# One block of GLA, NSA and SwiGLU: buffers of FFN and down projection laid at 160 and 224 modulo 256, plain weight tiles by token halves, and single products cut in two

## The chip, the cores and the metric

The kernel runs on one core of one Trainium2 chip. The metric is the device time of one execution in microseconds; the number used is the median of three runs.

## The reference, cut to what matters

One decoder block over x with 512 tokens and 1024 features, in float32:

```python
h = rms_norm(x, norm_mix_pre)
proj = h @ w_in                       # split into GLA q, k, v, r, a; NSA q, k, v; gates; merge gates
o_gla, o_nsa = gla_mixer(...), nsa_mixer(...)
mixed = sigmoid(merge_gla) * (o_gla @ w_proj_gla) + sigmoid(merge_nsa) * (o_nsa @ w_proj_nsa)
x = x + rms_norm(mixed @ w_out, norm_mix_post)
h = rms_norm(x, norm_ffn_pre)
f = (silu(h @ w_ffn_gate) * (h @ w_ffn_up)) @ w_ffn_down      # 1024 -> 2816 -> 1024
x = x + rms_norm(f, norm_ffn_post)
```

GLA is a chunked gated linear attention with 4 heads, NSA an attention with 8 heads over compressed blocks, selected blocks and a window. Neither changes here.

## The kernel before, in words

All activations lie transposed, features on the 128 partitions and the 512 tokens along the free dimension. The dense products run in float32r with a split: each weight and each activation is a high part and a low part (`whi`, `wlo`; `hT_hi`, `hT_lo`), and one block of 128x128 weights gives three matmuls, high by high, high by low, low by high, summed in a PSUM bank. Below, "product" is one such matmul.

**Plain tiles.** A tile of 128 output features is eight blocks k = 0 to 7 of 128 input features, so 24 products, each over all 512 tokens (`prod`, lines 177 to 186). These are: eight tiles of q, k and merge gates at the start (`qa`, from `with_gla`), run in pieces of one block with side work between; six of `with_cmp`; 19 of `with_att`, which are fed into the gaps of the attention; the tile T_MB+7; eight tiles `pb` of half the depth (12 products); output projection tiles 0 to 2; gate and up tile 2 of the FFN (`third`); and eight tiles of the down projection over its last eight blocks of hidden features, with bank `acc` and `tp` in turn and the forms of the next stage as side work (`side`).

**By halves already.** Output tiles 3 to 7 (`out_half`) and gate and up tiles 0 and 1 (`ffn_half`) run for 256 tokens at a time.

**Units.** The other dense layers use a 2x2 scheme with seven instead of eight block products (Strassen's, in Winograd's form): nine pairs of input tiles (`eproduct`), 19 units of gate and up tile n = 3 to 21 (`unit`, N0 = 3), and four units of the down projection over 14 blocks (`down_product`). Their products are all 256 columns wide: 12 in each of the seven block products of a pair or a unit, 21 in those of down. The sums of weight quarters and of token halves, and their split into high and low parts (`dform`, `x_form`, `split_pair`), are DVE's and ACT's work beside the products.

**What sets the order.** The code calls the steps in a hand-made order; a scheduler then orders each engine's instructions by readiness and the code's order, so products of neighbouring steps may be interleaved. Each engine runs its own queue in order. PSUM has banks of four names (`mm`, `sc`, `acc`, `tp`), two of each; a bank is free when the engine that evacuates it is done. Weights come by DMA on SP's queue into `wraw`, are split by ACT and DVE, and one tile ahead is asked for (`Stream`).

**Where buffers lie.** SBUF pools hand out addresses one after the other, in the order of the requests. A tile of 16 floats (`half_line`) shifts all that follows by 64 bytes. "At 160" means that a buffer's address in its partition is 160 modulo 256 bytes. Before, `hT` and the inputs of pairs and units begin at 160 and their weights at 224, except for some buffers of FFN and down: the two last parts of `h2l`, `t2` and parts of `b11` and `t1` of down lie at 224 as moving operands, and the weights of output tile 7 and `u2` (`w_e`) lie at 160.

Of the kernel before, what the change touches and what calls it, by code (L numbers as in the profile page):

```python
# [16 lines left out]
S = 512  # L17
# [77 lines left out]
def hybrid_block_kernel(ctx: ExitStack, tc: tile.TileContext, I, outT):  # L95
# [78 lines left out]
    ALL = slice(0, S)  # L174

    def prod(ps, w, xh, xl, k0, kn, ktot, t=ALL):

        wh, wl = w
        marks = []
        for kk in range(kn):  # L180
            k = k0 + kk
            c = slice(kk * 128, (kk + 1) * 128)
            pe.matmul(ps[:, t], wh[:, c], xh(k)[:, t], start=(k == 0), stop=False)  # L183
            pe.matmul(ps[:, t], wh[:, c], xl(k)[:, t], start=False, stop=False)  # L184
            marks.append(pe.matmul(ps[:, t], wl[:, c], xh(k)[:, t], start=False, stop=(k == ktot - 1)))  # L185
        return marks
# [39 lines left out]
    halves = (slice(0, S // 2), slice(S // 2, S))  # L226
# [86 lines left out]
    def eplace(u, a):  # L313
# [5 lines left out]
        if a == "a22" and u + 1 < NU:  # L319
            if u == 0:  # L320
                half_line(mid)
            return [mid.tile([128, S], F32R, tag="kst" + x, name="ek" + x) for x in "sw"]
# [56 lines left out]
    def eproduct(u, i):  # L379
# [11 lines left out]
        for q in range(4):  # L391
            c = slice(q * 128, (q + 1) * 128)
            for m, (w, x) in enumerate(((wh, xh), (wh, xl), (wl, xh))):
                pe.matmul(o, w[:, c], x[q], start=(first and q == 0 and m == 0), stop=(q == 3 and m == 2),  # L394
                          skip_group_check=True)
# [288 lines left out]
    class Pieces:  # L684


        def __init__(self, keys):
            self.it = (None for key in keys for _ in self.one(key))

        def one(self, key):  # L690
# [79 lines left out]
    qa = Pieces(with_gla)  # L770
# [6 lines left out]
    gates_log(AF.Exp, stk["abs"], scale=-1.0)  # L777
    first = pair(0, (15, 16), (3, 5))
# [12 lines left out]
    mid2 = p_mid2.__enter__()  # L791
    p_nsa = tc.tile_pool(name="nsa", bufs=1, reuse_waits="tile")
# [334 lines left out]

    weave(runs(with_cmp[:2]), [])
# [13 lines left out]
    mix2 = p_mix2.__enter__()  # L1142
    run(("h", T_MB + 7))
# [28 lines left out]
    early = [flat(quad("e%d" % i, F32, "early%d" % i)) for i in range(2)]  # L1172

# [3 lines left out]
    def w_slot(which):  # L1177
# [4 lines left out]
        tags = {"d0": ("d0h", "d0l"), "d1": ("d1h", "d1l"), "c": ("hl2", "hl3"), "u": ("uu", "uu"), "g3": ("g3h", "g3l"), "rw": ("rw", "rw")}[which]  # L1182
# [5 lines left out]
    rs = []  # L1188

    def w_e():  # L1190
        if not rs:
            rs.append(ffn.tile([128, 48], F32, name="rs3"))
# [4 lines left out]
    h2h, h2l = quads("h2h", 4, F32R, "hh"), quads("h2l", 2, F32R, "hl")  # L1197
    rs1, rs2 = [ffn.tile([128, NT], F32, name=x) for x in ("rs1", "rs2")]
    h2l += [quad("hl%d" % i, F32R, "h2l%d" % i) for i in (2, 3)]
# [72 lines left out]
    def ffn_half(e, w, ps, ks=range(KD)):  # L1272
# [3 lines left out]
        for k in ks:  # L1276
            i, j = k // 2, k % 2
            c = slice(k * 128, (k + 1) * 128)
            for x in range(2):
                wh, wl = w[x]  # L1280
                o = ps[x][:, t]
                pe.matmul(o, wh[:, c], h2h[i][:, j, t], start=(k == 0), stop=False)
                pe.matmul(o, wh[:, c], h2l[i][:, j, t], start=False, stop=False)
                last = pe.matmul(o, wl[:, c], h2h[i][:, j, t], start=False, stop=(k == KD - 1))
# [144 lines left out]
    def unit(n, between=None):  # L1429
# [7 lines left out]
        def product(o, a, b, first):  # L1437
            (ah_, al_), (bh_, bl_) = forms.pop((n, a)), XF[b]
            for q in range(4):
                c = slice(q * 128, (q + 1) * 128)  # L1440
                for i, (w, x) in enumerate(((ah_, bh_), (ah_, bl_), (al_, bh_))):
                    pe.matmul(o, w[:, c], x[q], start=(first and q == 0 and i == 0), stop=(q == 3 and i == 2),  # L1442
                              skip_group_check=True)
# [13 lines left out]

        product(r1, "a11", "b11", True)
# [36 lines left out]
    def dform(name, room_for, src, t):  # L1495
        cols = [x if len(x.shape) == 2 else flat(x) for x in room_for]
        at = [x[:, c:c + 512] for x in cols for c in range(0, x.shape[1], 512)]
# [18 lines left out]
    half_line(ffn)  # L1516
    w0 = (st.next(("g", 0)), st.next(("u", 0)))
    for n in BYHALF:
# [77 lines left out]
    with tc.issue_after(stk["last"].ins):  # L1596
# [7 lines left out]
    dform("b11", [quad("sa", F32R, "db11_%d" % i) for i in range(2)] + [quad("rw", F32R, "db11_%d" % i) for i in (2, 3)],  # L1604
          left, h0)
    t2d = [quad("g3h", F32, "dt2_0"), quad("g3l", F32, "dt2_1")]
    for i in range(4):
        dve.tensor_tensor(out=half_of(t2d, i), in0=left(i, h1), in1=left(i, h0), op=OP.add)
# [8 lines left out]
    def sub_t2(of, t, by):  # L1617
        for i in range(4):
            dve.tensor_tensor(out=of(i, t), in0=by(i, t if by is of else h1), in1=half_of(t2d, i), op=OP.subtract)

    side = [
        lambda: dform("t2", [quad("hl2", F32R, "dt2h0"), quad("hl3", F32R, "dt2h1"),
                             quad("uu", F32R, "dt2l0"), quad("uu", F32R, "dt2l1")], t2_of, None),
        lambda: sub_t2(left, h0, right),
        lambda: dform("t3", [quad(x, F32R, "dt3" + x) for x in ("e0", "e1", "hl0", "hl1")], left, h1),
        lambda: dform("t1", [quad(x, F32R, "dt1" + x) for x in ("e2", "e3", "d1h", "d1l")], left, h0),
        lambda: dform("b21", [base.tile([128, S], F32R, tag="b%d" % i, name="db21_%d" % i) for i in range(4)]
                      + [quad("a%d" % i, F32R, "db21l%d" % i) for i in (0, 1)], right, h0),
# [4 lines left out]
    draw, dw = {}, {}  # L1633

    def dload(u, q):
        if u >= 4:
            return
        tag = ("a3" if q == "12" else "wraw") if u < 3 else "hh%d" % ("12", "22", "21", "11").index(q)
        raw = (wts.tile([128, 1024], F32, tag="wraw", bufs=3, name="wraw") if tag == "wraw"
               else flat(quad(tag, F32, "raw" + q)))  # L1640
# [4 lines left out]
    def dsum(u, name):  # L1645
        r11, r12, r21, r22 = [draw[u, q] for q in ("11", "12", "21", "22")]
        if name == "s2":
            dve.tensor_tensor(out=r21, in0=r11, in1=r21, op=OP.subtract)
            x = flat(quad("a2", F32, "raws2"))[:, :KW]
# [28 lines left out]
    y2q = [quad("d0" + x, F32, "y2_" + x) for x in "hl"]  # L1678
# [198 lines left out]
```

## Time and profile before

| what | value |
|---|---|
| median of 3 runs | 849.33 us (848.9 to 850.09) |
| profiled execution, its own time | 849.72 us |
| span of the profiled execution | 847.8 us |
| mean granted TensorE clock | 0.995 |
| HBM read, written | 102.21 MB, 4.19 MB |

The span runs from the first to the last instruction; the execution's own time is 1.9 us more. In the span, the input norm and the token-major projection take the first 68 us or so, the plain tiles and pairs follow to 205, the rest of GLA, the plain tiles of `with_cmp` and the attention with its fill to 426, T_MB+7, `pb` and the output projection to 502, gate and up to 720, the plain down tiles to 766, and the down units and the end to 848.

How to read it: durations of matmuls in the groups overlap those of their neighbours, since they are pipelined; the distance from start to start says how fast products follow each other. In a window of time the number behind x counts each instruction that touches it.

### The profile page before, as it was taken

The page shows a single profiled execution, that of the slowest core. Times are in us where ns is not written, and L with a number is a line of the kernel's source. Part 1 is how long each engine was busy: PE and PEld are TensorE (multiplying, and loading weights), DVE is VectorE, ACT ScalarE, POOL GpSimd, SP SyncE. Part 2 cuts the span into 40 slices and gives each one's busy share as a digit, 9 for nine tenths or more (in the row PEclk, how much of TensorE's full clock was granted, in tenths as well). Part 3 has the DMA queues.
Part 4 walks back from the last instruction along what each step waited for, and adds up shares of the span by engine and source line. Part 5 has one row for each costly group of instructions (what it writes and reads, how often), then busy time and mean ns, then how long its engine had stood idle before and what let it go on. Part 6 is the DMA issues. An engine that isn't in the chain of part 4 may idle for free.

```text
span 847.8 us, 14724 instructions
## 1 busy us (share of the span) xinstructions
PE 832.0 (98%) x5592; PEld 758.5 (89%) x5592; DVE 631.9 (75%) x1206; ACT 526.3 (62%) x964; POOL 144.7 (17%) x174
## 2 busy tenths in 40 slices
PE   9999999999999999999999999999999999999995
PEld 8998899999888788888878999999999999789995
DVE  7766896874366778877667468998888779739886
ACT  6547767664463888888645576866665567435441
POOL 0101022221040100010000355211121110001443
PEclk9999999999999999999999999999999999999998
DMA  8343465773241454545327749698878882325323
GB/s 281 96 118 89 114 123 127 152 155 96 75 157 51 100 115 109 124 100 116 72 63 239 257 137 247 123 218 230 204 181 197 198 184 63 104 83 174 87 101 100
DMA packets 41095, 117.86 MB, mean 139 GB/s; under 512 B 4700, under 2 KB 6764, under 8 KB 40896
## 3 DMA queue, kind: packets, MB, share of 16 engines
q1 hardware_dynamic: 27808, 82.49, 31.1%
q0 software_dynamic: 12496, 33.88, 21.8%
q8 instruction: 44, 0.72, 0.3%
q10 hardware_dynamic: 720, 0.54, 0.2%
q14 instruction: 27, 0.22, 0.1%
HBM read 102.21 MB, written 4.19 MB: 126 GB/s over the span
## 4 chain that ended last, share of the span: by engine, by line
PE 85%; ACT 4%; DVE 4%; issue 3%; DMA 2%; POOL 1%; SPq 0%; ACTq 0%; POOLq 0%; DVEq 0%
PE ps_mm L183 6%; PE ps_mm L185 6%; PE ps_mm L184 6%; PE ps_mm L394 6%; PE ps_mm L1442 6%; PE ps_tp L1442 6%; PE ps_acc L1442 5%; PE ps_sc L1442 4%; PE ps_sc L1730 4%; PE ps_acc L1730 2%; PE ps_mm L1730 2%; PE ps_tp L1038 2%; PE ps_acc L183 1%; PE ps_acc L184 1%; PE ps_acc L185 1%
## 5 line engine op out<-in xcount | busy, mean ns | idle before, releaser
L59 ACT CAST whi<-wraw 128x1024 fp32r<-128x1024 f32 (+2 forms) x63 | 61.2, 973 | 70.8 <-PE ps_mm L184 18.7
L183 PE MATMUL ps_mm<-hT_hi,whi 128*128 128x512 f32 x200 | 81.6, 408 | 0.0
L66 DVE TENSOR_TENSOR wlo<-wraw,whi 128x1024 fp32r<-128x1024 f32 (+2 forms) x48 | 52.6, 1095 | 38.5 <-ACT whi L59 36.1
L184 PE MATMUL ps_mm<-hT_lo,whi 128*128 128x512 f32 x200 | 79.4, 397 | 0.0
L185 PE MATMUL ps_mm<-hT_hi,wlo 128*128 128x512 f32 x200 | 79.0, 395 | 0.0
L185 PEld LDWEIGHTS ps_mm<-hT_hi,wlo 128*128 128x128 f32 x200 | 37.6, 188 | 9.1 <-DVE wlo L66 0.3
L183 PEld LDWEIGHTS ps_mm<-hT_hi,whi 128*128 128x128 f32 x200 | 37.6, 188 | 7.8
L184 PEld LDWEIGHTS ps_mm<-hT_lo,whi 128*128 128x128 f32 x200 | 37.7, 188 | 6.7
L201 DVE TENSOR_TENSOR pl<-ps_tp,ph 128x512 fp32r<-128x512 f32 (+1 forms) x64 | 31.1, 489 | 14.7 <-ACT ph L200 14.1
L998 ACT ACTIVATE p<-p,mx 128x512 f32<-128x512 f32 (+1 forms) x64 | 35.9, 561 | 8.9 <-DVE mx L996 8.4
L996 DVE CUSTOM_DVE_ANT_0 p<-ps_sc,causal 128x512 f32<-128x512 f32 (+1 forms) x64 | 30.2, 486 | 11.0 <-PE ps_sc L989 10.6
L63 POOL DMA_DIRECT2D wlo<-wraw x15 | 12.7, 850 | 150.1 <-ACT wlo L62 90.6
L200 ACT CAST ph<-ps_tp 128x512 fp32r<-128x512 f32 (+1 forms) x64 | 26.5, 415 | 4.4 <-PE ps_tp L1038 3.9
L394 PE MATMUL ps_mm<-hT_hi,feq 128*128 128x256 f32 x144 | 27.3, 282 | 1.4 <-DVE qst L398 0.6
L1038 PE MATMUL ps_tp<-ident,p 128*128 128x128 f32 x160 | 27.9, 272 | 0.0
L1038 PEld LDWEIGHTS ps_tp<-ident,p 128*128 128x128 f32 x160 | 20.8, 140 | 7.2 <-ACT pc L927 0.3
L1339 POOL DMA_DIRECT2D wlo<-in_w_gate x13 | 11.5, 885 | 77.2 <-ACT wlo L1337 77.1
L1355 ACT CAST w_hl<-s 128x1024 fp32r<-128x1024 f32 x12 | 12.5, 1045 | 19.3 <-PE ps_acc L1442 9.0
L394 PEld LDWEIGHTS ps_mm<-hT_hi,feq 128*128 128x128 f32 x144 | 22.7, 188 | 2.0 <-DVE qst L398 0.8
L1355 ACT CAST w_d0h<-s 128x1024 fp32r<-128x1024 f32 x13 | 13.6, 1044 | 16.5 <-PE ps_mm L1442 6.8
L1355 ACT CAST w_d1h<-s 128x1024 fp32r<-128x1024 f32 x13 | 13.6, 1046 | 15.7 <-PE ps_mm L1442 7.8
L1007 DVE TENSOR_SCALAR p<-p,z 128x128 f32<-128x128 f32 (+1 forms) x64 | 20.4, 383 | 0.4
(875 smaller groups left out, 3232.9 us busy)
## 6 DMA issues: line engine op xcount, KB each, us to landing
wraw<-in_w_t SPq DMA_DIRECT2D x36, 512.0 KB, 3.7
wraw<-in_w_gate SPq DMA_DIRECT2D x21, 512.0 KB, 4.3
rw<-in_w_up SPq DMA_DIRECT2D x19, 512.0 KB, 7.9
wlo<-wraw POOLq DMA_DIRECT2D x15, 512.0 KB, 4.5
wlo<-in_w_gate POOLq DMA_DIRECT2D x13, 512.0 KB, 8.3
wraw<-in_w_tok SPq DMA_DIRECT2D x12, 440.0 KB, 3.4
w_uu<-in_w_up POOLq DMA_DIRECT2D x19, 256.0 KB, 8.7
wraw<-in_w_proj SPq DMA_DIRECT2D x8, 512.0 KB, 3.6
```

What stands on the lines that cost most here:

```text
L59: self.nc.scalar.copy(hi[:, :cols], raw[:, :cols])
L66: self.nc.vector.tensor_tensor(out=lo[:, :cols], in0=raw[:, :cols], in1=hi[:, :cols].bitcast(F32), op=OP.subtract)
L183: pe.matmul(ps[:, t], wh[:, c], xh(k)[:, t], start=(k == 0), stop=False)
L184: pe.matmul(ps[:, t], wh[:, c], xl(k)[:, t], start=False, stop=False)
L185: marks.append(pe.matmul(ps[:, t], wl[:, c], xh(k)[:, t], start=False, stop=(k == ktot - 1)))
L201: dve.tensor_tensor(out=lo, in0=src, in1=hi.bitcast(F32), op=OP.subtract)
L394: pe.matmul(o, w[:, c], x[q], start=(first and q == 0 and m == 0), stop=(q == 3 and m == 2), skip_group_check=True)
L998: act.activation(out=o, in_=o, func=AF.Exp, scale=-1.0, bias=mx[:, i:i + 1], accum_out=z[:, i:i + 1])
L1038: pe.transpose(tp[:, i * 128:(i + 1) * 128], p[:, OFF[i] + k * 128:OFF[i] + (k + 1) * 128], ident)
L1355: act.copy(hi, t)
L1442: pe.matmul(o, w[:, c], x[q], start=(first and q == 0 and i == 0), stop=(q == 3 and i == 2), skip_group_check=True)
L1730: pe.matmul(o, w[:, c], x[q], start=(first and q == 0 and i == 0), stop=(q == KH - 1 and i == 2), skip_group_check=True)
```

## The change

It has four parts.

1. A plain tile (`prod` without a given range of tokens) is computed as two halves of 256 tokens, one whole half after the other; in `qa`, a piece is now two blocks of one half (`by_half`). The tiles fed into the attention stay 512 wide, and so does gate tile 2, which is called with its depth in two parts.
2. All split products go through one helper, `three`. After a call of `restart()`, the next product group of 256 columns has its second product, high by low, cut into two of 128 columns, with the same weights. The nine calls stand ahead of: the `qa` tiles, pair 0, the `with_cmp` tiles, T_MB+7, the output halves, unit N0, unit N0+3, the plain down tiles, the down units.
3. Buffers of FFN and down are blocks of 2048 or 2112 floats (`double`), so that nearly all moving operands lie at 160 and the weights at 224. `u2` and output tile 7 keep their weights at 160. The tiles of the attention shift by 192 bytes (`gap_mid2`).
4. In the down section the plain tiles use banks `mm` and `sc` (first four) and `acc` and `tp` in turn, and the forms `b11` and the sum `t2` move into the side work of the first plain tile; several buffers there have other places.

```diff
+    def restart():
+        fresh[0] = True
+
+    def three(o, w, x, start, stop):
+
+        (wh, wl), (xh, xl) = w, x
+        n = o.shape[1]
+        pe.matmul(o, wh, xh, start=start, stop=False, skip_group_check=True)
+        cut = [slice(0, 128), slice(128, 256)] if fresh[0] and n == 256 else [slice(0, n)]
+        if n == 256:
+            fresh[0] = False
+        for c in cut:
+            pe.matmul(o[:, c], wh, xl[:, c], start=False, stop=False, skip_group_check=True)
+        return pe.matmul(o, wl, xh, start=False, stop=stop, skip_group_check=True)
+
+    def prod(ps, w, xh, xl, k0, kn, ktot, t=None):
+
+        if t is None and kn == ktot:
+            return [prod(ps, w, xh, xl, k0, kn, ktot, half) for half in halves][-1]
+        t = ALL if t is None else t
...
-            pe.matmul(ps[:, t], wh[:, c], xh(k)[:, t], start=(k == 0), stop=False)
-            pe.matmul(ps[:, t], wh[:, c], xl(k)[:, t], start=False, stop=False)
-            marks.append(pe.matmul(ps[:, t], wl[:, c], xh(k)[:, t], start=False, stop=(k == ktot - 1)))
+            marks.append(three(ps[:, t], (wh[:, c], wl[:, c]), (xh(k)[:, t], xl(k)[:, t]), k == 0, k == ktot - 1))
...
-            for k in range(KD):
-                prod(ps, [x[:, k * 128:(k + 1) * 128] for x in w], xh, xl, k, 1, KD)
-                if k + 1 < KD:
+            for i in range(KD):
+                if self.by_half:
+                    k, kn, t = 2 * i % KD, 2, halves[2 * i // KD]
+                else:
+                    k, kn, t = i, 1, ALL
+                prod(ps, [x[:, k * 128:(k + kn) * 128] for x in w], xh, xl, k, kn, KD, t)
+                if i + 1 < KD:
...
+    mid2.tile([128, 48], F32, name="gap_mid2")
...
+    def double(tag, dtype=F32R):
+
+        return ffn.tile([128, 2112 if tag == "c" else 2048], dtype, tag=tag, bufs=1, name=tag + "_two")
+
+    h2c = double("c")
+    h2l += [h2c[:, 48 + 1024 * i:48 + 1024 * (i + 1)].rearrange("p (a t) -> p a t", a=2) for i in range(2)]
...
-        tags = {"d0": ("d0h", "d0l"), "d1": ("d1h", "d1l"), "c": ("hl2", "hl3"), "u": ("uu", "uu"), "g3": ("g3h", "g3l"), "rw": ("rw", "rw")}[which]
+        if which in ("d0", "d1", "c"):
+            t = double(which)
+            return t[:, 0:1024], t[:, 1024:2048]
+        tags = {"u": ("uu", "uu"), "g3": ("g3h", "g3l"), "rw": ("rw", "rw")}[which]
...
+        if n in (N0, N0 + 3):
+            restart()
         product(r1, "a11", "b11", True)
...
-    half_line(ffn)
     w0 = (st.next(("g", 0)), st.next(("u", 0)))
+    restart()
     for n in BYHALF:
...
     side = [
-        lambda: dform("t2", [quad("hl2", F32R, "dt2h0"), quad("hl3", F32R, "dt2h1"),
-                             quad("uu", F32R, "dt2l0"), quad("uu", F32R, "dt2l1")], t2_of, None),
+        lambda: dform("b11", [quad("sa", F32R, "db11_%d" % i) for i in range(2)] + [shifted("d0")], left, h0),
+        sum_t2,
+        lambda: dform("t2", [base.tile([128, S], F32R, tag="b%d" % i, name="dt2_%d" % i) for i in range(8)], t2_of, None),
...
-        lambda: dform("t1", [quad(x, F32R, "dt1" + x) for x in ("e2", "e3", "d1h", "d1l")], left, h0),
-        lambda: dform("b21", [base.tile([128, S], F32R, tag="b%d" % i, name="db21_%d" % i) for i in range(4)]
-                      + [quad("a%d" % i, F32R, "db21l%d" % i) for i in (0, 1)], right, h0),
+        lambda: dform("t1", [quad(x, F32R, "dt1" + x) for x in ("e2", "e3")] + [shifted("d1")], left, h0),
+        lambda: dform("b21", [quad("a%d" % i, F32R, "db21_%d" % i) for i in range(4)], right, h0),
...
+    restart()
     for n in range(8):
-        ps = bank("acc" if n % 2 == 0 else "tp")
+        ps = bank(("mm", "sc", "acc", "tp")[n % 2 + n // 4 * 2])
         prod(ps, sd.next(("d", n)), fh, fl, 0, KP, KP)
         act.copy(y2[n], ps)
-        if n < len(side):
-            side[n]()
+        for f in (side[0:2], side[2:3], side[3:4], side[4:5], side[5:6], side[6:7], side[7:8], [])[n]:
+            f()
...
     for j, (u, a, b) in enumerate(seq):
+        if j == 0:
+            restart()
         end = down_product(j)
```

What this makes of PE's order is seen at two places. A row is a line of the code (L183 to L185 the three products of `prod` before; L186, L191, L192 those of `three` after), the operation, the tile written, the tiles read, and the shape; x2 is the same row twice. First, the place where the last unit ends (its forms are `x_2` and `x_3`, its bank `acc`) and the plain down tiles begin. Before:

```order
L1442 MATMUL ps_acc<-x_2_5842,w_d1h 128x256
L1442 MATMUL ps_acc<-x_3_5843,w_d1h 128x256
L1442 MATMUL ps_acc<-x_2_5842,w_d1l 128x256
L183 MATMUL ps_tp<-hT_hi,whi 128x512
L183 MATMUL ps_acc<-hT_hi,whi 128x512
L184 MATMUL ps_acc<-hT_lo,whi 128x512
L185 MATMUL ps_acc<-hT_hi,wlo 128x512
L183 MATMUL ps_acc<-hT_hi,whi 128x512
```

After, with the cut, and further on the end of the first half of plain tile 0, where the last block k = 7 of `hT` is used:

```order
L191 MATMUL ps_acc<-x_3_6399,d_two 128x256
L192 MATMUL ps_acc<-x_2_6398,d_two 128x256
L186 MATMUL ps_mm<-hT_hi,whi 128x256
L191 MATMUL ps_mm<-hT_lo,whi 128x128 x2
L192 MATMUL ps_mm<-hT_hi,wlo 128x256
...
L191 MATMUL ps_mm<-hT_lo,whi 128x256
L192 MATMUL ps_mm<-hT_hi,wlo 128x256
L186 MATMUL ps_sc<-hT_hi,whi 128x256
L191 MATMUL ps_sc<-hT_lo,whi 128x256
L192 MATMUL ps_sc<-hT_hi,wlo 128x256
L186 MATMUL ps_mm<-hT_hi,whi 128x256
L186 MATMUL ps_sc<-hT_hi,whi 128x256
```

The 512-wide products in `tp` and `acc` have become 256-wide ones in `mm`, the second cut in two. The first half's eighth block stands behind three products of the next tile (`ps_sc`), as its single row `ps_mm<-hT_hi` shows, and the rest of its block nine products later.

Second, the cut at unit N0+3, whose first product is `ps_sc<-hT_lo,whi`; around it stand products of units N0+1 and N0+2 (`ps_mm`, `ps_acc`). After:

```order
L186 MATMUL ps_sc<-hT_hi,whi 128x256
L191 MATMUL ps_sc<-hT_lo,whi 128x128
L186 MATMUL ps_mm<-hT_hi,d_two 128x256
L191 MATMUL ps_mm<-hT_lo,d_two 128x256
...
L191 MATMUL ps_acc<-x_3_6399,c_two 128x256
L192 MATMUL ps_acc<-x_2_6398,c_two 128x256
L191 MATMUL ps_sc<-hT_lo,whi 128x128
L192 MATMUL ps_sc<-hT_hi,wlo 128x256
```

One of the two 128-column parts stands between products of unit N0+1, the other 121 rows further on, behind the last rows of `x_3` in unit N0+2; at the other eight places the two parts follow each other.

More of the change, by code (lines that the diff above doesn't have):

```diff
@@ L320, in eplace @@
             if u == 0:
+                for i in (2, 3):
+                    mid.tile([128, S], F32, tag="qst%d" % i, name="place")
                 half_line(mid)
@@ L392, in eproduct @@
             c = slice(q * 128, (q + 1) * 128)
-            for m, (w, x) in enumerate(((wh, xh), (wh, xl), (wl, xh))):
-                pe.matmul(o, w[:, c], x[q], start=(first and q == 0 and m == 0), stop=(q == 3 and m == 2),
-                          skip_group_check=True)
+            three(o, (wh[:, c], wl[:, c]), (xh[q], xl[q]), first and q == 0, q == 3)
         def add(out, y):
@@ L1172, in hybrid_block_kernel @@
     early = [flat(quad("e%d" % i, F32, "early%d" % i)) for i in range(2)]
+    places = [quad(tag, F32, "place") for tag in ("e2", "e3")]
+    h2h, h2l = quads("h2h", 4, F32R, "hh"), quads("h2l", 2, F32R, "hl")
+    places.append(quad("sa", F32, "place"))
+    rs12 = ffn.tile([128, 2 * NT], F32, name="rs12")
+    rs1, rs2 = rs12[:, 0:NT], rs12[:, NT:2 * NT]
+    rs3 = ffn.tile([128, NT], F32, name="rs3")
+    def double(tag, dtype=F32R):
+        return ffn.tile([128, 2112 if tag == "c" else 2048], dtype, tag=tag, bufs=1, name=tag + "_two")
+    h2c = double("c")
+    h2l += [h2c[:, 48 + 1024 * i:48 + 1024 * (i + 1)].rearrange("p (a t) -> p a t", a=2) for i in range(2)]
     def wtile(tag):
@@ L1281, in ffn_half @@
                 o = ps[x][:, t]
[L1282 to L1284 removed]
+                last = three(o, (wh[:, c], wl[:, c]), (h2h[i][:, j, t], h2l[i][:, j, t]), k == 0, k == KD - 1)
             marks.append(last)
@@ L1440, in product @@
                 c = slice(q * 128, (q + 1) * 128)
-                for i, (w, x) in enumerate(((ah_, bh_), (ah_, bl_), (al_, bh_))):
-                    pe.matmul(o, w[:, c], x[q], start=(first and q == 0 and i == 0), stop=(q == 3 and i == 2),
-                              skip_group_check=True)
+                three(o, (ah_[:, c], al_[:, c]), (bh_[q], bl_[q]), first and q == 0, q == 3)
         def add(out, ps, b):
@@ L1633, in hybrid_block_kernel @@
     draw, dw = {}, {}
+    two_raw = double("c", F32)
     def dload(u, q):
@@ L1728, in down_product @@
             c = slice(q * 128, (q + 1) * 128)
-            for i, (w, x) in enumerate(((wh, xh), (wh, xl), (wl, xh))):
-                pe.matmul(o, w[:, c], x[q], start=(first and q == 0 and i == 0), stop=(q == KH - 1 and i == 2),
-                          skip_group_check=True)
+            three(o, (wh[:, c], wl[:, c]), (xh[q], xl[q]), first and q == 0, q == KH - 1)
         if a == "a11":
```

52 lines of the change are left out of this document (28 added, 24 removed).

## The prediction

> **What bounds the kernel now.** I read the page first: the span, the busy shares, the chain that ended last.
>
> ```profile
> span 847.8 us, 14724 instructions
> ...
> PE 832.0 (98%) x5592; PEld 758.5 (89%) x5592; DVE 631.9 (75%) x1206; ACT 526.3 (62%) x964; POOL 144.7 (17%) x174
> ...
> PEclk9999999999999999999999999999999999999998
> ...
> PE 85%; ACT 4%; DVE 4%; issue 3%; DMA 2%; POOL 1%; SPq 0%; ACTq 0%; POOLq 0%; DVEq 0%
> ```
>
> TensorE is busy in 98% of the span at an even, full clock, and makes up 85% of the chain. DVE is at 75%, but it stands in the chain for 4% alone. So the time is, nearly, the number of products times the distance from one start to the next. The durations in the groups don't give that distance (a 512-wide product of line 183 is printed with 408 ns, because the records of neighbours overlap); it has to be taken from stretches in which nothing else runs. Next, therefore, the busy time by windows, cut where one kind of product stands alone (us, PE busy with the number of matmuls that touch the window, clock, DMA share, GB/s; the count has one or two that started before it):
>
> ```profile
> core 0: us, PE busy (x), PEclk, DMA share, GB/s
> 437.25:453.83 16.58, 16.58 (x74) 1.00 0.49 139
> 459.59:470.79 11.20, 11.20 (x49) 1.00 1.00 387
> 470.79:482.10 11.31, 11.31 (x98) 1.00 0.74 241
> 482.10:484.98 2.88, 2.88 (x27) 1.00 0.84 238
> 500.00:526.00 26.00, 25.50 (x219) 1.00 0.70 188
> 537.94:548.54 10.60, 10.60 (x92) 1.00 0.31 60
> 566.84:719.95 153.11, 153.11 (x1353) 1.00 0.76 182
> 732.05:765.65 33.60, 33.60 (x146) 1.00 0.28 85
> 765.65:828.00 62.35, 62.30 (x534) 1.00 0.38 123
> 768.15:770.66 2.51, 2.51 (x23) 1.00 0.76 234
> ```
>
> What to see: 512-wide products (plain tiles) take 33.60/144 = **233.3 ns** in the plain down tiles, 11.20/48 = 233.3 in out tiles 0 to 2, 16.58/72 = 230 in the eight `pb` tiles. 256-wide products, half the columns, have two paces that last: **113.3 ns** (153.11 us for some 1351 in the units from N0+1 on) and **117.8 ns** (11.31/96 in the out halves, 10.60/90 at the first unit). Neither DMA traffic nor the clock sorts them: the fast one runs at a DMA share of 0.76, the slow one at 0.31 and 0.74. A third value depends on where the operands lie. A buffer's place, its address in the partition modulo 256 bytes, follows from the sizes that the pools gave out before it. Where moving operand and weights both begin at 160 (out tile 7, 2.88 us for 24) a product takes 120 ns, where both begin at 224 (down's `t2`, 2.51 us for 21) 119.5. All the others named lie at 160 with weights at 224, and have either of the two paces.
>
> The arithmetic of the change is in this: a 512-wide product is 233.3; two halves are 2x113.3 = 226.7 (6.7 ns won), at the slow pace 235.6 (2.3 lost), with like places 240 (6.7 lost).
>
> **How a pace is taken up.** The timeline of PE (start, duration, line, tiles) where out tile 2 gives way to the halves, without a wait:
>
> ```profile
> 470.33 0.40 PE L184 MATMUL ps_mm<-hT_lo,whi 128*128 128x512 f32 x1
> 470.56 0.39 PE L185 MATMUL ps_mm<-hT_hi,wlo 128*128 128x512 f32 x1
> 470.79 0.28 PE L183 MATMUL ps_sc<-hT_hi,w_rw 128*128 128x256 f32 x1
> 470.91 0.28 PE L184 MATMUL ps_sc<-hT_lo,w_rw 128*128 128x256 f32 x1
> 471.03 0.28 PE L185 MATMUL ps_sc<-hT_hi,w_rw 128*128 128x256 f32 x1
> ```
>
> The slow pace stands from the first halves and stays to the next interruption. Behind narrow products (one column, 128 columns) it comes out either way, two stretches of the same out tiles:
>
> ```profile
> 490.99 0.58 PE L208 MATMUL ps_tp<-ones,sqh 128*128 128x1 f32 x4
> 491.44 0.36 PE L183 MATMUL ps_mm<-hT_hi,w_d0h 128*128 128x256 f32 x1
> ...
> 494.25 0.60 PE L221 MATMUL ps_tp<-ident,rs 128*128 128x128 f32 x4
> 494.62 0.36 PE L183 MATMUL ps_mm<-hT_hi,w_d1h 128*128 128x256 f32 x1
> 494.82 0.28 PE L184 MATMUL ps_mm<-hT_lo,w_d1h 128*128 128x256 f32 x1
> ...
> 491.99:494.22 2.23, 2.23 (x22) 1.00 0.52 206
> 495.18:502.35 7.17, 7.17 (x63) 1.00 0.57 143
> ```
>
> About 113 ns behind the first, 117.5 behind the second. Of twelve such places five took the fast pace. So the trace shows that a narrow product can change the pace; it doesn't show that it always sets the fast one. That is the main unknown.
>
> **The change, part by part.** Four parts: (1) 744 products of 512 columns become 1488 of 256 (8 `qa` tiles, 6 of `with_cmp`, T_MB+7, out tiles 0 to 2, `u2`, the 8 plain down tiles, 24 products each but for the 8 `pb` tiles' 12); (2) the buffers of FFN and down are laid so that nearly everything is at 160 with weights at 224; (3) nine products are cut into two of 128 columns; (4) in the down section banks and side work are ordered anew.
>
> (1) With all at the fast pace 744x6.7 = 5.0 us, with all at the slow one -1.7. I take, by group: plain down 192 products, of 1.28 us 1.05 (one wait inside, see (4)); first four `qa` tiles 96, 0.4 of 0.64, since they run in pieces with waits between; last four, no cut ahead of them, the mean of both paces, 96x2.2 = 0.2; `with_cmp` 144, 0.4 of 0.96, woven with other work; T_MB+7 and out tiles 0 to 2, 96, and `pb`, 96 at only 230-226.7 = 3.3, together 0.6 of 0.95; `u2` keeps moving operand and weights both at 160, so 24x-6.7 = -0.15. Sum **2.5 us**.
>
> (2) Products that are 256 wide already. Down units: 62.35/534 = 116.8 on average, so 534x3.5 = 1.85 above the fast pace, because `t2` and parts of `t1` and `b11` lie at 224 and the heads fall slow; I take 1.3. Out halves 96x4.5 = 0.45 (out tile 7 stays at 120). FFN halves, 26.00 us with 25.50 busy, have two of four low parts at 224; 0.3. Unit N0's first 90 at 117.8 would be 0.4 less; 0.35. The early pairs, where waits decide each time anew, 0.15. Sum **2.55 us**. Between 0 and the full excess of some 4.5 us.
>
> (3) A cut adds one product. Nearest row: four of 128 columns and the first 256-wide one fill 494.25 to 494.82, 0.57/5 = 0.114 us each, as much as a 256-wide one. So nine cuts cost 9x0.114 = **1.0 us**; the lower end is 0 (two halves stream no more columns than one), and below nothing only through the pace, which stands in (1) and (2). Nothing hides this, TensorE being the path.
>
> (4) The start of the plain down tiles, PE, then DVE and ACT:
>
> ```profile
> 719.95 0.39 PE L183 MATMUL ps_tp<-hT_hi,whi 128*128 128x512 f32 x1
> 720.98 0.50 PE L183 MATMUL ps_acc<-hT_hi,whi 128*128 128x512 f32 x1 [0.64 <-DVE wk L1446]
> ...
> 720.51 0.41 DVE L1446 TENSOR_TENSOR wk<-ps_acc,us 128x256 f32<-128x256 f32 x1
> ...
> 723.05 0.41 DVE L1456 TENSOR_TENSOR slot<-sl,wk 128x256 f32<-128x256 f32 x1
> ...
> 724.92 0.68 DVE L201 TENSOR_TENSOR hT_lo<-slot,hT_hi 128x512 fp32r<-128x512 f32 x1
> ...
> 723.76 0.62 ACT L200 CAST hT_hi<-slot 128x512 fp32r<-128x512 f32 x1
> ```
>
> One product starts at 719.95, the next 1.03 us later: 0.8 us lost on bank `acc`, which the last unit still holds. With `mm` and `sc` first, that wait goes. What is late next is block k=7, the last unit's own output: `hT_hi` of it is cast from 723.76, `hT_lo` subtracted from 724.92. Before, k=7 came 21 products of 512 later, 720.98+21x0.233 = 725.9, behind both. Now the first half reaches it after 21 of 256 and the cut, 719.95+22x0.113 = 722.4, and three products of `ps_sc` bring it to 722.8; then one product of `ps_mm` needs `hT_hi`, ready at 724.2 or so. All the rest of PE's queue stands behind it, 1.4 us. Nine `ps_sc` products then cover `hT_lo` (to 725.3). DVE's row of work there (wk, slot, side forms, slot, forms, `hT_lo`) is the same length as before, so I don't move it earlier. Net 1.4-0.8 = **0.6 us lost**, from 0.8 won (all is ready) to 2 lost (side forms ahead of the last casts). The forms of `b11` and the sum `t2`, eight to ten DVE operations of 0.3 to 0.7 us, now stand beside the plain down tiles:
>
> ```profile
> core 0: us, PE busy (x) PEld busy (x) DVE busy (x) ACT busy (x) POOL busy (x), PEclk, DMA share, GB/s
> 720.00:765.65 45.65, 45.01 (x195) 36.05 (x193) 26.35 (x39) 19.84 (x34) 0.00 (x0) 1.00 0.29 87
> ```
>
> DVE has 19 us free there and ACT 25, so I cost them at nothing; ahead of the last casts they would be the 2 us above. The loads of the down units' weights are issued beside plain tile 6, as before, into other buffers that are free by then: nothing, and the DMA share of 0.29 says the same.
>
> Sum: 2.5+2.55-1.0-0.6 = **3.45 us**. The profiled execution took 849.72 us, so 846.3; it is 0.39 above the median 849.33, for which I say **845.9 us**.
>
> The rule that speaks against the change: the Trainium skill, "TensorE: Matmul & The Clock Gate", section "Back-to-back issue gap", gives a matmul of N columns N/2.4 ns and about 2.5 ns on top. By it, an estimate from that page, 512 columns are 215.8 ns and two halves 218.3, a loss of 1.9 us over 744 products. The trace disagrees with both figures (233.3, and 2x113.3 where the pace is fast). The same page, section "Step-by-step: what each phase is for", has two independent read ports for weights and moving operand; by it places could not matter and part (2) would lose the place's share, some 1.2 us; the 113.3, 119.5 and 120 ns above speak against it.
>
> **Rivals.**
> - *The cut doesn't set the pace*: each head falls as it did, half fast. Then (1) is 744x2.2 = 1.7, (2) is half the place effect, 1.2, less 1.6: 1.3 us won, **848.0**. For it: five of twelve. Against: the heads here are of one form.
> - *The cut sets the slow pace, or breaks the fast one, at unit N0+3*: in the stretch now at 113.3 throughout, the two 128-wide parts stand far apart in PE's order. From there to the plain down some 16 units of 84 = 1344 products would take 4.5 ns more, 6.0 us; the time is 849.3+6.0+1.6-2.5 = **854.4** with what part (1) brings, 856.9 without it. It decides at that one place: without a wait behind it, the pace holds for 150 us. For it: the slow stretch behind 494.25. Against: unit N0's own slow start became fast after waits by itself, and stayed.
> - *A fixed cost for each product*: halves pay one gap more, 2.3 ns by the slow pace's rows, places give nothing: 744x2.3 = 1.7, with 1.6 of (3) and (4) **852.6**. The gap that the Trainium skill states, above, would work like this; the 1351 at 113.3 speak against it.
> - *Everything fast*: 5.0-0.3+4.3-1.0+0.8 = 8.8 us, **840.5**. The many waits in the early pairs speak against it.
>
> **How the numbers follow.** Forecast (heads mostly fast) 0.57, everything fast 0.05, no set pace 0.20, slow at N0+3 0.13, fixed cost 0.05. Two runs of this kernel can be told apart from about 0.2%, 1.7 us: faster is below 847.6, slower above 851.0. Faster: 0.55+0.05+0.07 = 0.67. Same: 0.02+0.12+0.01 = 0.15. Slower: 0.01+0.12+0.05 = 0.18. The range from 841.0 to 851.5 takes in the forecast with its bounds, no set pace, and leaves out most of the slow case and the very best; faster cases alone are 841.0 to 847.6.
>
> **What would show it.** In the changed profile: windows of the plain down tiles at 113.3 for each product (33.60 us for 144 of 512 should become some 32.6 for 288), the units still 153 us for 1351, the down units near 114 on average, out tile 7 and `u2` at 120. The wait at the start of the plain down should name ACT `hT_hi` rather than DVE `wk`. I am wrong if the units' stretch is at 117.8, if the halves of plain tiles are at 117.8 although cut ahead of them, or if the wait for k=7 is over 2 us.

## The result, and the profile after

| kernel | median | runs | range |
|---|---|---|---|
| before | 848.9 us | 13 | 847.77 to 855.1 |
| changed | 858.98 us | 13 | 850.86 to 860.04 |

The change makes the kernel slower: ratio of the times 1.0096, 95% interval 1.0077 to 1.0116 (all runs; the medians differ by 1.2%). Two of the 13 runs of before lie at 853.5 and 855.1 us, the others at 847.8 to 850.1; two of the changed kernel lie at 850.9 and 854.0, the others at 856.5 to 860. Forecast were 845.9 us and a range that ended at 851.5.

The page of the changed kernel's profile, the lines that answer to those shown of before (its own execution took 859.7 us):

```profile
span 856.8 us, 16244 instructions
...
PE 837.6 (98%) x6345; PEld 796.7 (93%) x6345; DVE 633.0 (74%) x1206; ACT 526.5 (61%) x964; POOL 145.5 (17%) x174
...
PEclk9999999999999999999999999999999999999997
...
PE 76%; DVE 10%; ACT 7%; issue 4%; DMA 2%; POOL 1%; SPq 0%; ACTq 0%; DVEq 0%; POOLq 0%
```

PE is busy 98% as before and the clock is full, so the page alone says only that TensorE's own work has become longer, by 5.6 us. DVE and ACT, busy as long as before, stand in the chain with 17% instead of 8%: more of it now runs through work that TensorE waits for. The windows of PE say where (us, busy with the number of matmuls touched, clock, DMA share, GB/s):

```profile
core 0: us, PE busy (x), PEclk, DMA share, GB/s
433.00:454.00 21.00, 21.00 (x188) 1.00 0.41 123
533.77:539.05 5.28, 5.28 (x46) 1.00 1.11 206
540.00:542.40 2.40, 2.40 (x23) 1.00 0.58 114
570.71:728.10 157.39, 157.39 (x1339) 1.00 0.75 177
731.69:773.90 42.21, 42.21 (x360) 1.00 0.25 71
774.80:785.90 11.10, 11.10 (x101) 1.00 0.77 274
804.00:829.00 25.00, 25.00 (x214) 1.00 0.33 103
```

The fourth row is the loss. The units from N0+3 to the plain down tiles, at 113.3 ns before, now take 157.39/1337 = 117.7 ns a product. The first row (`pb` by halves), the third (unit N0) and the sixth (the first down units) are at the fast pace, the second (`u2`) at 120 as forecast; the plain down tiles, 42.21/358 = 117.9, and the last down units are slow.

By stages, as lengths from the first product of one to the first of the next, read from the starts of the products in the traces (the profiled run of before reached the first `qa` tile at 68.25 us, all others in this study at 66.0 to 66.6, so lengths are compared, not starts; e2, g2 and g0 are the experiments of these names below):

| stage | before | changed | e2 | g2 | g0 |
|---|---|---|---|---|---|
| `qa` head to first `pa` tile | 179.6 | 181.7 | 181.6 | 179.3 | 179.3 |
| to `pb` (attention) | 183.9 | 184.7 | 184.6 | 184.6 | 184.2 |
| to unit N0 | 106.2 | 106.4 | 105.9 | 105.2 | 106.3 |
| units, to the plain down | 182.0 | 188.9 | 183.7 | 183.1 | 182.6 |
| plain down tiles | 45.7 | 45.8 | 44.7 | 46.3 | 45.7 |
| down units, to the last product | 74.0 | 74.5 | 73.4 | 74.4 | 74.0 |

6.9 us are lost in the units and 2.1 in the first stage; no stage is shorter than before. Each column is one profiled run. That of e2 took 850.65 us, the shortest of its nine, so its lengths may be on the low side.

The timeline of PE at the place where the pace turns (start, duration, line, tiles, shape):

```profile
569.80 0.28 PE L191 MATMUL ps_acc<-x,c_two 128*128 128x256 f32 x1
569.91 0.28 PE L192 MATMUL ps_acc<-x,c_two 128*128 128x256 f32 x1
570.03 0.22 PE L191 MATMUL ps_sc<-hT_lo,whi 128*128 128x128 f32 x1
570.08 0.33 PE L192 MATMUL ps_sc<-hT_hi,wlo 128*128 128x256 f32 x1
570.25 0.28 PE L186 MATMUL ps_sc<-hT_hi,whi 128*128 128x256 f32 x1
570.37 0.28 PE L191 MATMUL ps_sc<-hT_lo,whi 128*128 128x256 f32 x1
570.49 0.28 PE L192 MATMUL ps_sc<-hT_hi,wlo 128*128 128x256 f32 x1
```

Ahead of the lone half of the cut of unit N0+3 the starts are 0.113 us apart, behind it 0.118, and no wait comes until the plain down tiles. The two shortest runs of the changed kernel, at 850.9 and 854.0, were not profiled.

### The profile page after: what moved, and what is told of

The parts are those of the page before. It is cut to its first block, busy times and chain, and to the rows that moved or that the text cites. A ratio compares the mean times of both kernels' runs of the same rounds, so it can differ in the third digit from the quotient of the medians.

```text
span 856.8 us, 16244 instructions
## 1 busy us (share of the span) xinstructions
PE 837.6 (98%) x6345; PEld 796.7 (93%) x6345; DVE 633.0 (74%) x1206; ACT 526.5 (61%) x964; POOL 145.5 (17%) x174
## 4 chain that ended last, share of the span: by engine, by line
PE 76%; DVE 10%; ACT 7%; issue 4%; DMA 2%; POOL 1%; SPq 0%; ACTq 0%; DVEq 0%; POOLq 0%
PE ps_mm L186 11%; PE ps_mm L192 11%; PE ps_mm L191 11%; PE ps_sc L186 4%; PE ps_sc L191 4%; PE ps_sc L192 4%; PE ps_acc L186 3%; PE ps_acc L191 3%; PE ps_acc L192 3%; PE ps_tp L186 2%; PE ps_tp L191 2%; PE ps_tp L192 2%; PE ps_tp L1064 2%; DVE slot L1286 1%; PE ps_acc L1079 1%
## 5 line engine op out<-in xcount | busy, mean ns | idle before, releaser
L186 PE MATMUL ps_mm<-hT_hi,whi 128*128 128x256 f32 (+1 forms) x404 | 123.7, 307 | 0.3 <-ACT hT_hi L219 0.3
L192 PE MATMUL ps_mm<-hT_hi,wlo 128*128 128x256 f32 (+1 forms) x404 | 121.8, 302 | 0.2 <-DVE wlo L66 0.2
L191 PE MATMUL ps_mm<-hT_lo,whi 128*128 128x256 f32 (+2 forms) x407 | 121.0, 300 | 0.0
L186 PEld LDWEIGHTS ps_mm<-hT_hi,whi 128*128 128x128 f32 x404 | 76.3, 189 | 3.5 <-ACT hT_hi L219 0.4
L192 PEld LDWEIGHTS ps_mm<-hT_hi,wlo 128*128 128x128 f32 x404 | 75.9, 188 | 3.6 <-DVE wlo L66 0.4
L191 PEld LDWEIGHTS ps_mm<-hT_lo,whi 128*128 128x128 f32 x407 | 76.4, 189 | 1.8
L1390 ACT CAST d_two<-s 128x1024 fp32r<-128x1024 f32 x26 | 27.0, 1043 | 36.2 <-PE ps_mm L192 16.7
L1397 DVE TENSOR_TENSOR d_two<-s,d_two 128x1024 fp32r<-128x1024 f32 x25 | 30.6, 1223 | 11.6 <-ACT d_two L1390 11.6
L186 PE MATMUL ps_mm<-hT_hi,d_two 128*128 128x256 f32 x80 | 22.6, 283 | 0.0
L191 PE MATMUL ps_mm<-hT_lo,d_two 128*128 128x256 f32 x80 | 22.4, 279 | 0.0
```

The source lines that it names most:

```text
L186: pe.matmul(o, wh, xh, start=start, stop=False, skip_group_check=True)
L191: pe.matmul(o[:, c], wh, xl[:, c], start=False, stop=False, skip_group_check=True)
L192: return pe.matmul(o, wl, xh, start=False, stop=stop, skip_group_check=True)
L1390: act.copy(hi, t)
L1397: dve.tensor_tensor(out=lo, in0=t, in1=hi.bitcast(F32), op=OP.subtract)
```

## The experiments

Fourteen kernels ran. Theory A: two narrow products (of 128 columns) together set the fast pace, one alone turns it slow, a wait draws it anew. Its rivals: the places (B), chance alone (C).

**The cut at unit N0+3: taken away, put together, put alone into the kernel before; all cuts taken away.**

```diff
e1, e2 (to the changed kernel)
-        if n in (N0, N0 + 3):
+        if n == N0:
             restart()
         product(r1, "a11", "b11", True)
...
e2 alone
+        if n == N0 + 3:
+            restart()
         product(r2, "s2", "t2", True)
e3 (to the kernel before): unit N0+3's first x_lo product in two parts of 128
e4 (to the changed kernel)
     def restart():
-        fresh[0] = True
+        fresh[0] = False
```

> The changed kernel without the cut at unit N0+3 alone; all else as changed. Theory A (the lone 128-column product there turned the pace of the units slow): the stretch from unit N0+3 to the plain down runs at 113.3 ns again, 1341 x 4.5 ns = 6.0 us less, about 853 us. Theory B (the new places of the FFN buffers make the units slow): still 117.8 ns and about 859 us. Theory C (the pace is drawn at every interruption, whatever stands there): both paces over the runs, between 853 and 859.

> The cut of unit N0+3 moved from its first to its second block product, where the two 128-column parts follow each other in PE's order. Theory A, narrow form (a cut whose two parts stand together sets the fast pace, as at seven of the eight other heads; only the lone part is bad): 113.3 ns through the units, about 853 us in every run. Theory A, wide form (any cut at that place turns the pace slow): 117.8 ns, about 859 us. Theory B: about 859 us. Theory C: between 853 and 859, spread over the runs.

> The kernel before with nothing but one product cut in two at unit N0+3, where the two parts again stand some 55 rows apart. Theory A: the units' stretch falls to 117.8 ns and the time rises by 6 us to about 855. Theory B: no change, 849. Theory C: no change in most runs, since the kernel before is at about 849 in 11 of 13 runs and at 853 to 855 in two.

> The changed kernel without any of the nine cuts: halves, places, banks and side work as changed. Theory A: units as before at 113.3 ns in most runs, the heads of the plain tiles at either pace, slow behind 512-wide ones; without the 1.0 us of cuts but with slow heads 851 to 854 us. Theory B: about 858 us, the units at 117.8 ns. Theory C: spread over 850 to 859.

Measured: e1 856.2 us (852.15 to 858.12, 6 runs), e2 852.55 (850.65 to 854.68, 9 runs), e3 849.4 (847.57 to 854.66, 12 runs), e4 854.12 (851.14 to 857.76, 9 runs); the kernel before 848.87 beside them (23 runs). The units' stretch in their profiles, in this order:

```profile
568.00:721.50 153.50, 153.50 (x1356) 1.00 0.79 185
```

```profile
571.80:721.90 150.10, 150.10 (x1326) 1.00 0.78 182
```

```profile
565.00:724.60 159.60, 159.60 (x1358) 1.00 0.73 176
```

```profile
572.00:726.00 154.00, 154.00 (x1309) 1.00 0.75 176
```

113.4, 113.4, 117.7 and 117.8 ns. Theory B falls: e1 and e2 have the new places and the fast pace. e2 is 6.4 us faster than the changed kernel, and differs from it in the place of one cut. e1 and e4 show chance at work where no cut stands at unit N0+3, as theory C said of e1: their profiles fell one each way, and their runs spread over 6 us. e3 is a half miss: 855 in every run was expected, four of 12 came at 853 to 855. The timeline tells why:

```profile
563.46 0.22 PE L1444 MATMUL ps_sc<-hT_lo,whi 128*128 128x128 f32 x1
563.52 0.33 PE L1444 MATMUL ps_sc<-hT_hi,wlo 128*128 128x256 f32 x1
564.06 0.39 PE L1444 MATMUL ps_acc<-x5h,w_uu 128*128 128x256 f32 x1 [0.21 <-DVE us L1448]
```

Here PE waits right behind the lone part (0.54 us from start to start, released by DVE), and the pace is drawn again.

**What keeps the rest 3.7 us above before: cuts behind the waits (e5), the attention's places (e6), the first tiles whole (e7); and the cuts without the change (e8).**

```diff
e5 (to e2): restart() ahead of pb tiles 1 and 4, output tile 1, plain down tiles 2 and 5,
  in place of those at T_MB+7 and the first plain down tile
-        if j == 0:
+        if j in (0, 4, 7, 11, 14, 18, 22):
             restart()
e6 (to e2)
-    mid2.tile([128, 48], F32, name="gap_mid2")
e7 (to e2): the with_cmp tiles 512 wide, too
-    qa = Pieces(with_gla, True)
-    restart()
+    qa = Pieces(with_gla)
e8 (to the kernel before): three() in units, output tiles and down, cuts at the output halves
  and (parts together) at unit N0+3
+        fresh[0] = j in (2, 4, 8, 11, 15, 18, 22)
         end = down_product(j)
```

> The kernel with the cut of unit N0+3 together, and the cuts of T_MB+7, the plain down tiles and the down units moved behind the places where a wait undoes them (pb tiles 1 and 4, output tile 1, plain down tiles 2 and 5, every third or fourth block product of down; 17 cuts instead of nine, 0.9 us more). Theory A (two narrow products together set the fast pace, a wait behind them draws it anew): pb to the end at 113.3 ns in every run, the spread from run to run shrinks to under 2 us, about 850.5 us. Rival D (what is left over the kernel before is not pace but waits that take up every gain): no better than 852.5.

> The kernel with the cut of unit N0+3 together, without the 192 bytes that shift the attention's tiles. Theory E (the shifted places cost the attention stage time: it was 0.7 us longer than before in the profile): 0.7 us less, about 851.8. Rival: the stage is longer for the halves of the six tiles ahead of it, no change, 852.5.

> The kernel with the cut of unit N0+3 together, but the eight tiles at the start and the six of with_cmp whole again (512 columns), without the cuts there. Theory D (the first 250 us are set by DVE and ACT, and TensorE waits out what it wins): no loss, 852.5 or up to 1 us less. Rival (the halves pay there as in the sum, 1.2 us): 853.7.

> The kernel before (its places, its 512-wide tiles, its order) with cuts whose parts stand together: at the output halves, at unit N0+3's second block product, and at seven block products of down. Theory A: the units at 113.3 ns in every run (no more single runs at 853), the output halves 0.5 us less, down 1.0 less for 0.8 of cuts: 848.0 to 848.5 us. Rival C (the pace is drawn whatever is cut): as before, 848.9 with single runs at 853, plus 1.0 us of cuts.

Measured over 12 runs each: e5 852.76 us (851.5 to 855.26), e6 853.03 (850.22 to 856.31), e7 **849.55** (847.54 to 850.7), e8 851.75 (850.72 to 856.29); before 848.75 (35 runs). e6: the attention's places are worth nothing that can be seen. e7: the halves of the first tiles don't pay, they cost 3.0 us. e5 and e8 are misses of theory A's sizes, in the same stage: with the pace set again and again, down takes 75.1 us in e5 and 77.5 in e8, against 73.4 in e2 and 74.0 in before. (e7, whose down section is that of e2, takes 75.8, so the number of e5 alone proves little.) PE's waits from the plain down tiles or the down units to the end (waited for, total us, times, longest), first of before, then of e5, then of e8:

```profile
PE ps_tp L221 <- POOL rs L215: 1.1, 1, 1.1
PE ps_acc L183 <- DVE wk L1446: 0.6, 1, 0.6
```

```profile
PE ps_sc L186 <- DVE y L1756: 1.6, 1, 1.6
PE ps_tp L240 <- POOL rs L234: 1.1, 1, 1.1
```

```profile
PE ps_sc L181 <- DVE y_h L1720: 1.6, 2, 1.0
PE ps_tp L232 <- POOL rs L226: 1.1, 1, 1.1
PE ps_acc L181 <- DVE wk L1455: 0.6, 1, 0.6
PE ps_mm L181 <- DVE us L1720: 0.2, 1, 0.2
```

The loss lies at these `ps_sc` products, 12 to 17 us into the down units, where TensorE waits for DVE's adds: e5 is 0.2 us ahead of before after 105 products there, and 1.6 us behind after 126. The added cuts aren't needed for it, since e7 waits 1.3 us at the same place; why DVE is late there was not looked for. For e7, PE's waits from 66 to 247 us, e2's three largest and then e7's:

```profile
PE ps_mm L186 <- DVE eus L416: 1.6, 2, 1.0
PE ps_mm L186 <- ACT gq L751: 1.1, 1, 1.1
PE ps_mm L186 <- DVE gq L416: 0.7, 1, 0.7
```

```profile
PE ps_mm L187 <- DVE eus L417: 0.8, 1, 0.8
PE ps_mm L187 <- DVE gq L417: 0.7, 1, 0.7
PE ps_mm L187 <- DVE qst L417: 0.5, 1, 0.5
```

Two waits at pair 1 come with the halves, for ACT's copy of tile `gq`, 1.1 us, and for one of DVE's adds to `eus`, 1.0; e7 has neither there. The halves end the `qa` tiles at the same time (pair 1 starts at 100.98 us in e2, 101.14 in e7), but pair 1 then takes 12.6 us instead of 10.2. In the timelines of ACT and DVE the forms of its weights stand behind more of the GLA preparation: `feq` is cast at 101.95 instead of 101.11, and `gq`, behind it on ACT, copied at 102.99 instead of 102.15. The add waits for a weight load: with the halves, DVE's difference `erow` stands ahead of it, and DVE idles 2.15 us until `erow` has landed (at 107.84, 3.2 us after its issue). In e7 the add comes first, at 106.23, and `erow` at 107.17. In e2:

```profile
107.96 0.69 DVE L287 TENSOR_TENSOR erow<-wraw,erow 128x512 f32<-128x512 f32 x1 [2.15 <-DMA erow<-in_w_t]
```

All profiles agree on the size: the first stage takes 181.1 to 182.0 us in the seven with halves in `qa` and 179.0 to 179.7 in the nine without. e4 is one of the seven, at 181.9, so it is the halves and not their cuts.

**The pace by itself, and single parts of the change on the kernel before.**

```diff
g0 (to the kernel before): three() in the units
+        if n == N0 + 3:
+            fresh[0] = True
         product(r2, "s2", "t2", True)
f1 (to g0): at unit N0+5, in s2, the second part of the first x_lo product after nine others
+                    pe.matmul(o[:, ms], ah_[:, c], bl_[q][:, ms], start=False, stop=False, ...)
+                    if q == 3:
+                        pe.matmul(o[:, 128:256], ah_[:, 0:128], bl_[0][:, 128:256], start=False, ...)
g1 (to g0): cuts at the output halves and ahead of plain down tiles 2 and 5, and
-        ps = bank("acc" if n % 2 == 0 else "tp")
-        prod(ps, sd.next(("d", n)), fh, fl, 0, KP, KP)
+        ps = bank(("mm", "sc", "acc", "tp")[n % 2 + n // 4 * 2])
+        for half in halves:
+            prod(ps, w, fh, fl, 0, KP, KP, half)
g2 (to e2): as e7, but the with_cmp tiles stay by halves
```

> The kernel before with one cut alone, its two parts together, at unit N0+3's second block product. Theory A (two narrow products together set the fast pace, one alone the slow one, a wait draws it anew): every run at 113.3 ns through the units, 847.5 to 850 us, none at 853 to 855 as about one run in five of the kernel before; the median hardly moves, 848.7. Theory C (drawn whatever is cut): single runs at 853 again.

> The same, and two units later a cut whose two parts stand ten products apart, without a wait between them or behind them. Theory A: the first lone part turns the fast pace slow, and it stays so to the plain down tiles: some 16 units of 84 less two, 1150 products of 4.5 ns, 5.2 us more, about 854 us in every run. Rival F (a lone part only moves the phase, a second one moves it back): slow for ten products alone, 848.8. Rival C: as the kernel with one pair, 848.7.

> The kernel before with cuts together at unit N0+3 and the output halves, and of the change only the plain down tiles by halves with banks mm and sc first, cut at tiles 2 and 5. Theory A with D: 1.0 us less in the plain down tiles and 0.3 in the output halves, about 847.4 us. Rival (the down units' first forms, t4 and b22, are made after the plain tiles and PE waits for them, so the gain is given back there): 848.5.

> The kernel with the cut of unit N0+3 together, the eight tiles qa whole again and without cuts up to pair 0; the six tiles of with_cmp stay by halves. Theory G (the halves of qa move DVE's and ACT's order at pair 1, where TensorE waits 2.4 us more): the 3 us that the whole first tiles brought come from here, about 849.6 us. Rival: with_cmp's halves are the dear ones, 852.5.

Measured over 12 runs each: g0 **848.34** us (847.19 to 850.51), f1 849.48 (848.34 to 850.98), g1 849.48 (848.12 to 850.92), g2 849.85 (847.55 to 851.47); before 848.8 (35 runs, to 854.93). g2 is with e7: the dear halves are those of `qa`. g1's plain down tiles lose their bank wait and gain 0.6 us in the profile (45.07 against 45.69), and the down units behind them are 1.15 longer (75.10 against 73.95; h1, with the down units of before, has 75.2): the median shows no gain. In g0's profile the pair sets the fast pace out of the slow one. Its windows ahead of the cut and behind it:

```profile
549.50:567.30 17.80, 17.80 (x153) 1.00 0.84 212
568.50:718.00 149.50, 149.50 (x1322) 1.00 0.76 181
```

117.9 and 113.3 ns. f1 is a miss of theory A and a hit of rival F. Its windows ahead of the first lone part, between the two, and behind the second, under the usual columns:

```profile
570.00:587.50 17.50, 17.50 (x157) 1.00 0.91 236
587.92:588.90 0.98, 0.98 (x11) 1.00 0.68 217
590.00:719.60 129.60, 129.60 (x1146) 1.00 0.73 173
```

By the starts, 113.4 ns, about 117.8 (starts at 588.03 and 588.97, eight products apart) and 113.3. A second lone part led back, with the next four full distances still 0.118 to 0.120 us before the fast pace came.

**Whether that is a rule, and whether more cuts pay.**

```diff
h1 (to g0): cuts together also at the output halves and at unit N0
h2 (to the changed kernel): f1's second cut at unit N0+5
```

> The kernel before with three cuts, each with its two parts together: at the output halves, at unit N0 and at unit N0+3. If two narrow products together always set the fast pace: 0.4 us less in the output halves and up to 0.4 at unit N0, for 0.2 of cuts, so 847.8 us where one cut gave 848.34, and again no run at 853. If the waits behind unit N0's head take the gain up: 848.3.

> The changed kernel as it is, with its lone parts at unit N0+3, and two units later a second cut whose parts stand ten products apart. If a lone part leads from either pace to the other: 117.8 ns up to the first new part, 113.3 for the ten products between the parts, 117.8 behind them, 859 us. If a lone part leads to the slow pace from either: 117.8 throughout. If the second one of all heals what the first did: 113.3 from there on, 854 us.

h2: 857.39 us (3 runs). Its windows in the same order:

```profile
569.50:589.80 20.30, 20.30 (x175) 1.00 0.89 222
590.84:591.18 0.34, 0.34 (x6) 1.00 0.73 157
591.80:726.80 135.00, 135.00 (x1148) 1.00 0.73 170
```

By the starts, 117.8, 113 (0.34 us for the last three distances ahead of the second new part) and 117.8 ns: behind the changed kernel's lone part it is slow, the first new part leads to the fast pace, the second back to the slow one. The middle step is short here, since the first four full distances behind the first new part are still 0.117 to 0.122 us; f1 shows the same step over 1144 products. So a lone narrow product leads from either pace to the other. The profiles have seven such places without a wait right behind, in four kernels, five to the slow pace and two to the fast one.

h1: 849.32 us (847.28 to 855.09, 12 runs; before 849.16 beside it), a miss: four runs at 853 to 855. Its profile fell among them; the cut stands together, but a dozen products behind it PE waits a little, and the stretch after it is at 117.7 ns:

```profile
567.21 0.33 PE L186 MATMUL ps_sc<-hT_lo,w_d0h 128*128 128x128 f32 x2
...
568.81 0.33 PE L187 MATMUL ps_mm<-hT_hi,w_d1l 128*128 128x256 f32 x1
568.98 0.28 PE L181 MATMUL ps_mm<-hT_hi,w_d1h 128*128 128x256 f32 x1
```

```profile
569.50:723.80 154.30, 154.30 (x1312) 1.00 0.73 173
```

From 568.81 to 568.98 are 0.17 us instead of 0.113, and the pace behind it is the other one. The product at 568.81 is the first that takes `w_d1l`, and DVE had only just made it (it ends at 568.70; the weight load of the product starts at 568.75, 0.16 us behind the one ahead instead of 0.11):

```profile
567.49 1.21 DVE L1373 TENSOR_TENSOR w_d1l<-s,w_d1h 128x1024 fp32r<-128x1024 f32 x1
```

In g0, at the same cut, DVE ends it at 568.55 and its load starts at 568.85: no wait follows, and none of g0's 12 runs is slow.

## Why the prediction was wrong

**What bounds the kernel** was half right. TensorE is busy 98% in both kernels, and the two paces, 113.3 and 117.8, and 120 at like places, came back. But the sum took each product's pace as time, and the page's 98% hid that in three stages, the first pairs, the first units and the first down units, waits came or grew where TensorE was to gain. Of 5.0 us that parts (1) and (2) were to bring, no stage of the changed kernel shows any.

**The step that failed most** is the likeliest case, "heads mostly fast", at unit N0+3. The cut does set the fast pace where its two parts follow each other and no wait comes behind: in the profiles of this study wherever no wait came within the next dozen products and the operands lay at 160 and 224. At N0+3 the two parts stand 121 rows apart. There the lone part turns the pace, and it holds for 157 us: 1337 products by 4.4 ns, 5.9 us of the 6.9 lost in the units. That was the second rival, at 854.4 to 856.9 us, with its place and its price of 6.0; it was given 0.13. The measured 859.0 lies 2.1 above its upper end, about what the halves of `qa` cost, which no rival priced. The order showed the two parts apart before any run, and the trace of before showed narrow products lead both ways, so this case deserved far more than 0.13. The prediction weighed a cut that sets the fast pace against one that sets the slow pace; the runs show that the same cut does either, by whether its parts stand together and by the pace that it meets. Two of the signs that the prediction named for being wrong came true: the units' stretch at 117.8, and the plain down halves at 117.8 although cut ahead of them.

**Part (1)**, plain tiles by halves, forecast 2.5 us won. The `qa` tiles were to bring 0.6; they cost 2.7 to 3.0 in the medians (e2 to g2 and e7), since the changed order of ACT and DVE makes PE wait at pair 1. `pb` and the output tiles: from `pb` to unit N0 g2 takes 105.2 us against 106.2, but the seven profiles with this same code lie between 105.2 and 106.6, and four without it between 105.8 and 106.3, so no gain is shown. The plain down tiles: 1.0 us won in e2, e6 and e7 (44.7), as said, but nothing in the changed kernel, because the wait at k=7 comes behind the cut and the 358 products after it fell slow; in e1 and g2, slow there as well, they even lose 0.5 (46.2 and 46.3). `u2` was right.

**Part (2)**, 2.55 us: down was to gain 1.3. It gained 0.6 in e2, at the fast pace nearly throughout; but the seven profiles with this down section run from 73.0 (e6) to 75.8 us (e7), and five with that of before from 73.6 to 75.2, so no gain is shown here either. The units' first 90 products are fast as said, and the waits behind them grew instead: from 537 to 575 us the profile of before names none, that of e2 names one of 0.7 us for DVE and one of 0.2 for ACT.

**Part (3)** was right in size: in e2 the two parts and the product behind them fill 571.05 to 571.39 us, 0.34 instead of 0.227, 0.113 us for a cut:

```profile
571.05 0.33 PE L191 MATMUL ps_sc<-hT_lo,d_two 128*128 128x128 f32 x2
571.22 0.33 PE L192 MATMUL ps_sc<-hT_hi,d_two 128*128 128x256 f32 x1
571.39 0.28 PE L186 MATMUL ps_sc<-hT_hi,d_two 128*128 128x256 f32 x1
```

**Part (4)** was right in kind: the wait for bank `acc` went, and the one for ACT `hT_hi` of k=7 came:

```profile
730.94 0.28 PE L192 MATMUL ps_sc<-hT_hi,wlo 128*128 128x256 f32 x1
731.47 0.38 PE L186 MATMUL ps_mm<-hT_hi,whi 128*128 128x256 f32 x1 [0.25 <-ACT hT_hi L219]
```

It takes 0.53 us from start to start in the changed kernel, 1.0 in e2, where the products ahead of it are faster; 1.4 was said. Against the forecast the pace behind it cost more in the changed kernel: 358 products by 4.4 ns, 1.6 us, which the sum did not have.

**The fixed cost for each product** falls at the fast pace: the halves of `pb` take 2x113.3 = 226.6 ns where 512 columns took 230. At the slow pace two halves are 235.6 ns against 233.3, and a fixed cost of 2.3 ns would say the same, so there it isn't ruled out. The Trainium skill ("TensorE: Matmul & The Clock Gate", section "Back-to-back issue gap") states its gap of about 2.5 ns for isolated matmuls, not for streams of weight loads and matmuls like these; at the fast pace it doesn't show here.

**The balance**, in medians: from the changed kernel to the cut together 6.4 us (858.98 to 852.55), to whole `qa` tiles 2.7 (849.85), to before 1.0 (848.8; the same within its interval, ratio 0.9981, 0.9958 to 1.0003, which is over all runs, ten of the 35 of before at 853 to 855 among them). Two things stay open: why the attention stage is longer in all variants of the changed kernel, 184.3 to 184.7 us in nine profiles against 183.9 to 184.3 in the seven others (its places, in e6, are not the reason), and by which detail of a wait the pace is drawn.

The best kernel measured is g0, the kernel before with one cut: ratio 0.9981 (0.9961 to 1.0001), no different in the median, but 12 of 12 runs under 850.6, where ten of 35 of the kernel before beside it lay between 853.1 and 854.9. f1 and g1, with the same cut, add 24 runs, all under 851.0.

## What to carry to other kernels

A stream of weight loads and matmuls can have two lasting paces; find which by start-to-start distances, and look what stands at the last interruption ahead of the longest stretch, since that one place decides most. An instruction that is meant as one thing, such as a cut in two parts, has to be checked in the scheduled order, and against waits right behind it. A gain on a busy engine counts only in stages whose waits don't grow in its place: compare stages by their lengths, not by the engine's pace.

## What the runs showed of the hardware that was not expected

At operands at 160 and 224 modulo 256, a 128-column product alone in a stream of 256-column ones changes the pace from 113.3 to 117.8 ns or from 117.8 to 113.3 for all products up to the next interruption, over 1300 of them in the changed kernel. Two such products in a row left 113.3 from either pace (from 117.8 at g0's cut, from 113.3 at that of e2). A wait that made one distance 0.17 us instead of 0.113 was enough to change the pace in h1. The runs of before lie in two groups 5 to 6 us apart, at 847 to 851 and at 853 to 856 us. That such waits fall differently from run to run of one program is read from this, since each kernel has one profile: of before and its variants, those in the upper group (e3 at 853.36 us, h1 at 854.1) have the units at 117.7 ns, those in the lower one (before at 849.72, g0 at 848.15) at 113.3.
